# Lower query parts in both halves of the partitions, and score products over 128 rows, in a two-layer diffusion step on one Trainium2 core

## The chip, the core and the metric

The kernel runs on one core of one Trainium2 chip. The core has a matrix engine (TensorE; the profile calls its products PE and its weight loads PEld), a vector engine (DVE), a scalar engine (ACT), a general engine (POOL) and a queue engine (SP) that here issues nearly all transfers between the chip's memory and the core's on-chip memory. The on-chip memory has 128 partitions. The metric is the device time of one execution in microseconds (us).

## The reference: what is computed

One step of a small diffusion backbone in float32: 256 prompt tokens and 2048 sample tokens (a grid of 32 rows and 64 columns) with 1024 channels pass two layers. Layer 0 is a convolution branch, layer 1 an attention with 16 heads of 64 channels. The change touches the attention alone:

```python
# prompt: plain softmax attention of 256 tokens, per head
s = jnp.einsum('bqhd,bkhd->bhqk', qi, k).astype(jnp.float32)
p = jax.nn.softmax(s, axis=-1)
o = jnp.einsum('bhqk,bkhd->bqhd', p, v)

# sample: each block of 16 columns of a row sees 8 rows x 32 columns (a mask leaves 16) and 512 cached context keys
s_loc = jnp.einsum('bjqhd,brjkhd->bhjqrk', qb, k_blk)
s_loc = jnp.where(mask, s_loc + bias, NEG_INF)
s_ctx = jnp.einsum('bjqhd,blhd->bhjql', qb, k_ctx)
p = jax.nn.softmax(jnp.concatenate([s_loc, s_ctx], axis=-1), axis=-1)
o = p_loc @ v_blk + p_ctx @ v_ctx        # then gated by silu(z), projected, added to x, normalised
```

Every query is scaled by one over the root of 64, and the outputs are the two normalised activations and the prompt's new keys and values.

## The kernel before

**Numbers in two parts.** Products run in a float format that keeps fewer digits than float32. The kernel therefore splits an operand x into an upper part (x rounded to the format) and a lower part (what is left). A projection is three products: upper by upper, lower by upper, upper by lower.

For scores there are two products, because a head has only 64 channels and the array 128 rows. The keys of a head lie on all 128 partitions: the upper parts on 64, the lower parts on the other 64 (for odd heads the halves are exchanged). The upper parts of the head's queries, `hd.q`, are loaded from memory twice, into both halves of the partitions, so one product over 128 rows gives (upper queries) x (upper keys + lower keys). The lower parts of the queries, `hd.ql`, are loaded once for a pair of heads: the even head lies on partitions 0 to 63, the odd one on 64 to 127. The second product, line 1408, takes the 64 partitions of its head and the 64 partitions with the upper keys, and adds (lower queries) x (upper keys). In these products the queries are the weights that are loaded into the array, 128 queries at a time, and the keys stream through it.

**Stages.** Up to about 1800 us come the convolution layer and the projections of the attention layer (the queries' parts are written to memory as `qh_d` and `ql_d`). Then `phase2` does the attention. It goes twice over eight heads (a half); within a half first the prompt, two heads at a time (four prompt units), then four groups of eight grid rows, each with its eight heads. A sample head has four units of 128 queries (eight rows of one block of 16 columns). So there are 256 sample units and 8 prompt units.

**One unit** (`sample_unit`): scores against the 512 context keys (tile `ck`) and against a window of 11, 15, 15 or 12 key rows times 32 columns (tile `a_k`, read in a strided order; 352, 480, 480 or 384 columns), all into a score tile `sa_S` of which there are two; DVE takes the minimum and adds bias and mask (lines 1474 and 1476); ACT takes the exponential (1480), DVE the inverse of the sum (1481), POOL multiplies by it (1482); TensorE transposes the probabilities in eight pieces (1492); ACT copies them rounded (1501) and DVE forms the lower parts (109). Every second unit the value products follow (1517 to 1524), and between them, in pieces of six products, the output projection (1625 to 1627).

**Order.** `attention` runs the units as a pipeline. A step has the transposes of one unit, the softmax work of another, value products or a piece of the output projection, and then the scores of the next unit. TensorE and DVE keep the order in which the code is written (`manual_schedule`). ACT, POOL and SP are ordered by a scheduler with a time model of its own. `load_ahead` calls `load_head` one head ahead of use. The buffers that bear on this: keys `kt` two, upper queries `qh` two, lower queries `ql` two, bias `bm` two, values `vl` three. A load waits until the last reader of the buffer's former content is done, and SP issues its transfers one after the other, so a waiting one holds those behind it.

Of the kernel before, what the change touches and what calls it, by code (L numbers as in the profile page):

```python
# [52 lines left out]
# times of the start: of a weight's load, rounding and rest; of the first products; of the modulation; of the input rows  # L53
# [11 lines left out]
# per group of eight query rows: first key row, number of key rows  # L65
KEY_ROWS = [(0, 11), (4, 15), (12, 15), (20, 12)]
# and the key columns that share a product with the probabilities: ten where their rows fit the array, else eight
KEY_COLS = [10, 8, 8, 10]
# per block of 16 query columns: first key column / 8, kind of column window, first bias column
# [6 lines left out]
class Kern:  # L76
# [24 lines left out]
    # ---------------------------------------------------------------- helpers  # L101
# [15 lines left out]
    def slot(self, dt, name, shape, late=True):  # L117
        """16 KB per partition: of four that stay through phase 1 or of three that are given up before its end."""
        return self.sp.tile(shape, dt, tag="slot", name=name) if late else self.rp.tile(shape, dt, tag="slot", name=name, bufs=3)
# [10 lines left out]
    # -------------------------------------------------------------- constants  # L130
    def constants(self):
# [7 lines left out]
        # vectors over channels, one column per 128 channels  # L139
# [7 lines left out]
    def vectors(self, name, srcs, change=None):  # L147
        """Vectors over channels are loaded; the function returned puts them as columns of 128 channels."""
# [23 lines left out]
    def more_constants(self):  # L172
        """The other vectors, in two steps."""
        cp, io = self.cp, self.io
        columns = self.vectors("vecs", [io["norm_g"], io["ada_b"][0, : 2 * D]])
        yield
        vecs = columns()
        self.norm_g = [vecs[:, 0, :], vecs[:, 1, :]]
        self.ada_b = [vecs[:, 2, :], vecs[:, 3, :]]
        self.shift = [cp.tile([P, 2, NK], F32, tag=f"shift{i}", name=f"shift{i}") for i in range(2)]  # L180
        self.gs = [cp.tile([P, 2, NK], F32, tag=f"gs{i}", name=f"gs{i}") for i in range(2)]
        yield

    def conv_constants(self):
        """Depthwise taps, [channel, tap], in two steps."""
# [16 lines left out]
    def ada_chunk(self, i, c, late=True, early=False):  # L202
        """Columns c*512.. of the modulation of layer i for both groups, in steps: weights loaded, products (four at a
        time, each in its own 32 columns of the array), their sums, and the result put where it belongs."""
# [36 lines left out]
    def spread_row(self, tile, row):  # L241
        """A DRAM row on all partitions."""
# [3 lines left out]
    # ------------------------------------------------------------------- norm  # L246
# [38 lines left out]
    def modulated_steps(self, xts, layer, g, hi, lo, c0, name, rest, on_act=False, flush=(), wide=False):  # L285
        """Rows of xts (already scaled to unit rms), modulated, transposed and split, into columns c0.. of hi, lo."""
# [36 lines left out]
    # ------------------------------------------------------------ projections  # L323
    def weight(self, w, c0, name):
        """Columns c0..c0+128 of w, split."""
# [10 lines left out]
    def halves(self, src, shape, name):  # L336
        """A piece of a weight, rounded, and what is left of it."""
# [15 lines left out]
    # ------------------------------------------------------------- conv layer  # L353
    def conv_layer(self, part_a, part_b):
        """Input projection and depthwise convolution in two chunks of tokens; the second carries on where the first
        ends. Every operation is put at the time it is due by the tensor engine's rate, and all are issued in that
        order: the sums of the first taps of a channel tile run on Pool after its projection, those of the others on
        DVE after that. part_b are the blocks of the second chunk, made along the way."""
# [13 lines left out]
        for s in range(2 * NK):  # L372
# [93 lines left out]
            # the convolution, in two halves of the columns  # L466
# [48 lines left out]
            # the first half: Pool, then DVE in two sums; the second half: DVE, then Pool  # L515
# [28 lines left out]
        # the modulation and the input blocks of the first chunk  # L544
# [62 lines left out]
        # the norm of the first two tiles  # L607
# [13 lines left out]
        # the rest of the modulation, a part of it after each channel tile of the second chunk  # L621
# [5 lines left out]
        # the input blocks of the second chunk  # L627
# [38 lines left out]
    def norm_stages(self, src, t0, y, room=None, wide=False):  # L666
        """Layer norm, both SiLUs and their product of 128 tokens, in stages; appends split [channel, token] tiles to y.
        room has five [128, 8, 128] tiles to work in, for where the pools for that are not there yet."""
# [33 lines left out]
        # variance by token on the partitions, then its root's inverse spread over all partitions  # L702
# [34 lines left out]
    def out_weight(self, w, name, res):  # L737
        """w, split, as four tiles of 16 KB per partition: [hi, lo][half of the rows]; two steps for 128 rows."""
# [12 lines left out]
    def conv_out(self, w, blocks, ready, res=None):  # L751
        """Output projection and residual; with res also the modulated input of the next layer."""
# [43 lines left out]
    def conv_out_pipeline(self, w, blocks, ready, ahead, res):  # L796
        """Output projection, residual and modulated input of the next layer for blocks whose first tiles are ready;
        a step has the products of a tile, the first half of the norm of the second tile after it and the second half
        of the norm of the next one. Also the norm of the tiles ahead."""
# [127 lines left out]
    # -------------------------------------------------------- attention input  # L927
    def spread_bias(self):
        """The flat position bias, one copy per query of a tile, each shifted by the query's place in the bias."""
# [6 lines left out]
    def bias_rows(self, h):  # L936
        """Position bias of head h for every query of a tile, from row -4 and column -16 of the tile's first."""
# [4 lines left out]
    def na_values(self, blocks, then):  # L942
        """Values of some tokens, [token, channel]; then() where the weights that follow may be loaded."""
# [33 lines left out]
    def na_rest(self, blocks):  # L977
        """Keys, queries and gates of some tokens, [channel, token]."""
# [40 lines left out]
    def store_values(self, c, src, t0, pm):  # L1019
        """Values of four heads of 128 tokens as (hi, lo); those of the sample in the order (pair of columns, row, 2)."""  # L1020
# [21 lines left out]
    def masked_bias(self):  # L1042
        """Window mask less bias of every head, kind of row group and kind of column block: the scores are kept negated."""
# [20 lines left out]
    def windows(raw, at, R):  # L1064
        """[query, pair of columns, row, column]: 32 columns of R rows of the bias, which lie BIAS_COLS apart."""
# [3 lines left out]
    def store_q(self, dst, rows, src, t0, n, f):  # L1069
        """Columns of the sample are stored as (group of eight rows, j, row, 16)."""  # L1070
# [11 lines left out]
    def keys(self, ct, src, t0, n, pm, nm):  # L1082
        """Keys of two heads, stored as (hi, lo); those of odd heads as (lo, hi)."""
# [45 lines left out]
    def context_values(self):  # L1129
        """Cached values as (hi, lo)."""  # L1130
# [13 lines left out]
    def gated_weights(self):  # L1144
        """The weights of the last projection times the gate of either group, split."""
# [19 lines left out]
    # ------------------------------------------------------------------ phases  # L1165
    @staticmethod
    def weave(main, side, n):
        """main, with n steps of side (n may be a fraction) after each of its steps, and then the rest of side."""
# [53 lines left out]
    # ------------------------------------------------------- attention and out  # L1222
    def start_attention(self):
        """The pool of what heads load, and the loads of the first head."""
# [38 lines left out]
    def attention(self):  # L1263
        """All heads, as a pipeline of units: a step issues one stage of each of three units, sums of values or a part
        of the output projection, and what was put off from the steps before."""
# [69 lines left out]
    # ------------------------------------------------------------------- loads  # L1335
    def load_head(self, hd):
# [5 lines left out]
        if G is None:  # L1342
# [6 lines left out]
            hd.ql = T("ql", [P, n], F32R, nm + "_ql")  # L1349
            nc.sync.dma_start(hd.ql.bitcast(F32), self.ql_d[rows, a : a + n])  # L1350
# [14 lines left out]
        hd.q = T("qh", [P, n], F32R, nm + "_qh")  # L1365
        src = self.qh_d[h * DH : h * DH + DH, a : a + n]
        nc.sync.dma_start(hd.q.bitcast(F32), bass.AP(src.tensor, src.offset, [[0, 2], *src.ap]))
        if b == 0:
            hd.grp["ql"] = T("ql", [P, n], F32R, nm + "_ql")
            nc.sync.dma_start(hd.grp["ql"].bitcast(F32), self.ql_d[rows, a : a + n])  # L1370
        else:
            hd.z = T("z", [P, n], F32, nm + "_z")
            nc.sync.dma_start(hd.z, self.zn_d[rows, a : a + n])
        hd.ql = hd.grp["ql"]
# [3 lines left out]
    def load_context(self, ctx, h):  # L1378
        """The cached keys and values of a head."""
# [9 lines left out]
    def load_values(self, hd):  # L1389
        """The values of a head's key rows, in the chunks of the products."""  # L1390
# [13 lines left out]
    def scores(self, out, q, ql, k, odd):  # L1404
        """out = (hi + lo of the queries) times (hi + lo of the keys) without lo times lo."""
        half = slice(DH, P) if odd else slice(0, DH)
        self.nc.tensor.matmul(out, q, k, start=True, stop=False)  # L1407
        self.nc.tensor.matmul(out, ql[half], k[half], start=False, stop=True)  # L1408

    # ------------------------------------------------------------------- units  # L1410
    def prompt_unit(self, hd):
        """Softmax of the 256 prompt queries of two heads; transposed and split into hd.pt."""
# [322 lines left out]
```

## Time and profile before

| What | Value |
|---|---|
| median of 3 runs | 3113.68 us (3113.0 to 3121.12) |
| the profiled execution | its span, first to last instruction, is 3115.0 us, within the runs; nothing is recorded around it |
| PE, busy | 3005.0 us (96%) |
| PEld, busy | 2328.0 us (75%) |
| DVE, busy | 1857.6 us (60%) |
| ACT, busy | 1427.7 us (46%) |
| POOL, busy | 1538.2 us (49%) |
| transfers | 537.40 MB, mean 173 GB/s |
| products of line 1407, window | 256, mean 708 ns |
| products of line 1408, window | 256, mean 704 ns |

A row of the profile's groups names line, engine, operation, the tiles written and read, their shapes, the count, and the busy time. The digits of a shape such as 64*128 are the rows and columns of the array that a product uses. A row of the timeline gives start, duration, engine, line and operation. A product's end is modelled (products overlap in the array), so what a product costs is better read from one start to the next. "Issue" is idle time that no semaphore explains.

### The profile page before, as it was taken

The page shows a single profiled execution, that of the slowest core. Times are in us where ns is not written, and L with a number is a line of the kernel's source. Part 1 is how long each engine was busy: PE and PEld are TensorE (multiplying, and loading weights), DVE is VectorE, ACT ScalarE, POOL GpSimd, SP SyncE. Part 2 cuts the span into 40 slices and gives each one's busy share as a digit, 9 for nine tenths or more (in the row PEclk, how much of TensorE's full clock was granted, in tenths as well). Part 3 has the DMA queues.
Part 4 walks back from the last instruction along what each step waited for, and adds up shares of the span by engine and source line. Part 5 has one row for each costly group of instructions (what it writes and reads, how often), then busy time and mean ns, then how long its engine had stood idle before and what let it go on. Part 6 is the DMA issues. An engine that isn't in the chain of part 4 may idle for free. (4 is left out here: it accounts for less than half of the span.)

```text
span 3115.0 us, 45374 instructions
## 1 busy us (share of the span) xinstructions
PE 3005.0 (96%) x15951; PEld 2328.0 (75%) x15951; DVE 1857.6 (60%) x3126; ACT 1427.7 (46%) x2538; POOL 1538.2 (49%) x1775
## 2 busy tenths in 40 slices
PE   6999999998999999999999989999999999999998
PEld 4888877775778989999888856666666666666666
DVE  4789999988865000345652046656566656666665
ACT  4466566775533222422222145555555545555553
POOL 4688877886533433622333133444444444444443
PEclk9999999998999999999999979999999999999999
DMA  6242554564355544689998445755545456555442
GB/s 232 86 136 90 197 188 156 183 198 161 122 169 159 149 127 131 187 242 315 347 328 265 125 149 183 204 144 144 143 136 172 137 176 204 164 145 142 132 136 99
DMA packets 429373, 537.40 MB, mean 173 GB/s; under 512 B 42066, under 2 KB 304042, under 8 KB 429017
## 3 DMA queue, kind: packets, MB, share of 16 engines
q1 hardware_dynamic: 429008, 530.42, 55.0%
q10 hardware_dynamic: 136, 4.07, 0.3%
q8 instruction: 127, 2.08, 0.3%
q14 instruction: 102, 0.83, 0.1%
HBM read 351.34 MB, written 187.13 MB: 173 GB/s over the span
## 5 line engine op out<-in xcount | busy, mean ns | idle before, releaser
L1482 POOL TENSOR_SCALAR sa_p<-sa_p,sa_m 128x992 f32<-128x992 f32 (+2 forms) x256 | 288.2, 1126 | 528.9 <-DVE sa_m L1481 424.9
L1501 ACT CAST sa_pt<-sa_T 128x512 fp32r<-128x512 f32 (+2 forms) x512 | 276.0, 589 | 540.9 <-PE sa_T L1492 540.8
L500 DVE SCALAR_TENSOR_TENSOR cv<-u,dw,cv 128x640 f32<-128x640 f32 (+2 forms) x570 | 427.9, 822 | 3.8 <-ACT cv L496 2.9
L1474 DVE TENSOR_REDUCE sa_m<-sa_S 128x1 f32<-128x512 f32 x256 | 176.9, 691 | 403.3 <-PE sa_S L1408 390.1
L109 DVE TENSOR_TENSOR sa_pt<-sa_T,sa_pt 128x512 fp32r<-128x512 f32 (+2 forms) x512 | 329.2, 684 | 4.1 <-ACT sa_pt L1501 3.8
L349 PE MATMUL ci_ps<-h_s_hi,ci_wh 128*128 128x512 f32 x768 | 307.1, 400 | 2.0 <-DVE shift L237 1.0
L1492 PEld LDWEIGHTS sa_T<-ident,sa_p 128*128 128x128 f32 (+2 forms) x2048 | 221.5, 140 | 115.0 <-issue 57.3
L351 PE MATMUL ci_ps<-h_s_hi,ci_wl 128*128 128x512 f32 x768 | 303.2, 395 | 0.0
L350 PE MATMUL ci_ps<-h_s_lo,ci_wh 128*128 128x512 f32 x768 | 302.9, 394 | 0.0
L1492 PE MATMUL sa_T<-ident,sa_p 128*128 128x128 f32 (+2 forms) x2048 | 284.1, 282 | 0.9 <-DVE sa_pt L109 0.9
L1480 ACT ACTIVATE sa_p<-sa_S,sa_m 128x992 f32<-128x992 f32 (+2 forms) x256 | 269.4, 1052 | 7.6 <-DVE sa_m L1476 4.5
L481 POOL TENSOR_TENSOR cv_s<-cv_s,cv_p 128x519 f32<-128x519 f32 (+1 forms) x155 | 233.3, 1505 | 69.7 <-DVE cv_s L504 49.0
L478 ACT ACTIVATE cv_p<-u,dw 128x640 f32<-128x640 f32 (+2 forms) x326 | 240.9, 770 | 55.0 <-POOL cv_s L481 35.7
L481 POOL TENSOR_TENSOR cv_p<-cv_p,cv_p 128x520 f32<-128x520 f32 (+1 forms) x155 | 227.7, 1469 | 26.8 <-ACT cv_p L478 19.2
L1407 PE MATMUL sa_S<-a_k,a_qh 128*128 128x480 f32 (+2 forms) x256 | 181.3, 708 | 0.0
L1408 PE MATMUL sa_S<-a_k,a_ql 64*128 64x480 f32 (+2 forms) x256 | 180.3, 704 | 0.0
L1517 PE MATMUL sa_O<-sa_pt,cv 128*128 128x256 f32 x1024 | 177.1, 295 | 0.3 <-DVE 3_14_of L1538 0.3
L1476 DVE CUSTOM_DVE_ANT_0 sa_S<-sa_S,a_bm,sa_m 128x480 f32<-128x480 f32 (+2 forms) x256 | 170.9, 668 | 9.0
L349 PEld LDWEIGHTS ci_ps<-h_s_hi,ci_wh 128*128 128x128 f32 x768 | 145.5, 189 | 39.2 <-ACT cv_p L478 2.5
L351 PEld LDWEIGHTS ci_ps<-h_s_hi,ci_wl 128*128 128x128 f32 x768 | 145.1, 189 | 33.6
L350 PEld LDWEIGHTS ci_ps<-h_s_lo,ci_wh 128*128 128x128 f32 x768 | 145.4, 189 | 31.1
L106 POOL TENSOR_TENSOR nis_wl<-nis_w,nis_wh 128x1024 fp32r<-128x1024 f32 x24 | 60.9, 2540 | 183.0 <-ACT nis_wh L341 157.8
(846 smaller groups left out, 7495.5 us busy)
## 6 DMA issues: line engine op xcount, KB each, us to landing
adaw<-in_ada_w SPq DMA_DIRECT2D x24, 1024.0 KB
ci_w<-in_conv_w_in SPq DMA_DIRECT2D x48, 512.0 KB
a_bm<-bm_d SPq DMA_DIRECT2D x32, 720.0 KB
x_s<-in_x_sample SPq DMA_DIRECT2D x32, 512.0 KB
vs_d<-v_s SPq DMA_DIRECT2D x128, 128.0 KB
a_qh<-qh_d SPq DMA_DIRECT2D x64, 256.0 KB
o_x<-x_d SPq DMA_DIRECT2D x32, 512.0 KB
a_v<-vs_d SPq DMA_DIRECT2D x128, 120.0 KB
```

Of the source, the lines that this page charges most:

```text
L109: self.nc.vector.tensor_tensor(out=lo, in0=src, in1=hi.bitcast(F32), op=ALU.subtract)
L349: self.nc.tensor.matmul(out, wh[:, k, :], hh[:, k, :], start=k == 0, stop=False)
L350: self.nc.tensor.matmul(out, wh[:, k, :], hl[:, k, :], start=False, stop=False)
L351: self.nc.tensor.matmul(out, wl[:, k, :], hh[:, k, :], start=False, stop=k == NK - 1)
L478: nc.scalar.activation(t, st["u"][:, c0 + tap : c1 + tap], AF.Copy, scale=self.dw[:, ct, tap : tap + 1])
L481: nc.gpsimd.tensor_tensor(out=st["sum", half], in0=st["sum", half], in1=st[half, tap], op=ALU.add)
L500: nc.vector.scalar_tensor_tensor(out=out, in0=u, scalar=w, in1=first, op0=ALU.mult, op1=ALU.add)
L1407: self.nc.tensor.matmul(out, q, k, start=True, stop=False)
L1480: nc.scalar.activation(p[:, n], S[:, n], AF.Exp, scale=-1.0, bias=m[:, 2:3], accum_out=m[:, 3:4])
L1482: nc.gpsimd.tensor_scalar(out=p[:, n], in0=p[:, n], scalar1=m[:, 3:4], scalar2=1.0, op0=ALU.mult, op1=ALU.mult)
L1492: nc.tensor.transpose(t[:w, c * P : c * P + P], p[:, x + c * w : x + c * w + w], self.ident)
L1501: nc.scalar.copy(pt[:w, 0, part, :, at], t)
```

## The change

`load_head` now loads the lower parts of a head's queries as it loads the upper parts: twice, into both halves of the partitions, one tile per head. For the prompt, which takes two heads at once, the tile `ql` has two planes, and each head's plane is filled in both halves. `scores` no longer picks 64 partitions: its second product runs over all 128 rows, and gives (lower queries) x (upper keys + lower keys). The product of the two lower parts, which was left out before, is thereby included. The number of products, their columns and the weights' columns are as before; the tile `ql` takes the same space at most, 2 KB per partition. The load of the gate `hd.z` follows the load of `ql` for odd heads. The rest of the diff removes comments, which shifts line numbers by two from the loads on.

```diff
@@ load_head, prompt
-            hd.ql = T("ql", [P, n], F32R, nm + "_ql")
-            nc.sync.dma_start(hd.ql.bitcast(F32), self.ql_d[rows, a : a + n])
+            hd.ql = T("ql", [P, 2, NPR], F32R, nm + "_ql")
+            for e in range(2):
+                src = self.ql_d[(h + e) * DH : (h + e + 1) * DH, 0:NPR]
+                nc.sync.dma_start(hd.ql[:, e].bitcast(F32), bass.AP(src.tensor, src.offset, [[0, 2], *src.ap]))
@@ load_head, sample
-        hd.q = T("qh", [P, n], F32R, nm + "_qh")
-        src = self.qh_d[h * DH : h * DH + DH, a : a + n]
-        nc.sync.dma_start(hd.q.bitcast(F32), bass.AP(src.tensor, src.offset, [[0, 2], *src.ap]))
-        if b == 0:
-            hd.grp["ql"] = T("ql", [P, n], F32R, nm + "_ql")
-            nc.sync.dma_start(hd.grp["ql"].bitcast(F32), self.ql_d[rows, a : a + n])
-        else:
+        hd.q, hd.ql = (T(t, [P, n], F32R, f"{nm}_{t}") for t in ("qh", "ql"))
+        for t, d in ((hd.q, self.qh_d), (hd.ql, self.ql_d)):
+            src = d[h * DH : h * DH + DH, a : a + n]
+            nc.sync.dma_start(t.bitcast(F32), bass.AP(src.tensor, src.offset, [[0, 2], *src.ap]))
+        if b:
             hd.z = T("z", [P, n], F32, nm + "_z")
             nc.sync.dma_start(hd.z, self.zn_d[rows, a : a + n])
-        hd.ql = hd.grp["ql"]
@@ scores
-    def scores(self, out, q, ql, k, odd):
-        half = slice(DH, P) if odd else slice(0, DH)
+    def scores(self, out, q, ql, k):
         self.nc.tensor.matmul(out, q, k, start=True, stop=False)
-        self.nc.tensor.matmul(out, ql[half], k[half], start=False, stop=True)
+        self.nc.tensor.matmul(out, ql, k, start=False, stop=True)
@@ sample_unit (prompt_unit likewise)
-        self.scores(ctx, hd.q[:, cs], hd.ql[:, cs], hd.ctx[h][0], b)
-        self.scores(loc, hd.q[:, cs], hd.ql[:, cs], kw, b)
+        self.scores(ctx, hd.q[:, cs], hd.ql[:, cs], hd.ctx[h][0])
+        self.scores(loc, hd.q[:, cs], hd.ql[:, cs], kw)
```

TensorE's order stays as it was, and only the second products' weights are other tiles. The place is unit 0 of sample head 1 with the transposes around it; `a_0` and `a_1` are the tiles of heads 0 and 1. Before:

```order
L1407 MATMUL sa_1_0_S<-ck_16372,a_1_qh 128x512
L1408 MATMUL sa_1_0_S<-ck_16372,a_0_ql 128x512
L1407 MATMUL sa_1_0_S<-a_1_k,a_1_qh 128x352
L1408 MATMUL sa_1_0_S<-a_1_k,a_0_ql 128x352
L1492 MATMUL sa_0_2_T_17069<-ident,sa_0_2_p 128x128 x4
L1492 MATMUL sa_0_2_T_17074<-ident,sa_0_2_p 110x128 x4
```

After:

```order
L1405 MATMUL sa_1_0_S<-ck_16374,a_1_qh 128x512
L1406 MATMUL sa_1_0_S<-ck_16374,a_1_ql 128x512
L1405 MATMUL sa_1_0_S<-a_1_k,a_1_qh 128x352
L1406 MATMUL sa_1_0_S<-a_1_k,a_1_ql 128x352
L1490 MATMUL sa_0_2_T_17075<-ident,sa_0_2_p 128x128 x4
L1490 MATMUL sa_0_2_T_17080<-ident,sa_0_2_p 110x128 x4
```

The odd head reads a lower-query tile of its own, `a_1_ql`, where it read the even head's. DVE's order does not change at all; ACT and POOL each have one pair of neighbouring operations exchanged.

SP's order is rewritten by the scheduler. The place is the loads of sample head 4 in the second group of rows (`a_4_k` its keys, `a_4_bm` its bias, `a_4_v` its values). Before:

```order
L1364 DMA a_3_bm<-bm_d 128x1440
L1397 DMA a_3_v<-vs_d 30x8x128
L1370 DMA a_4_ql<-ql_d 128x512
L1397 DMA a_4_v<-vs_d 30x8x128 x2
L1359 DMA a_4_k<-ks_d 128x960
L1367 DMA a_4_qh<-qh_d 128x1x512
L1397 DMA a_4_v<-vs_d 30x8x128
L1364 DMA a_4_bm<-bm_d 128x1440
L1397 DMA a_4_v<-vs_d 30x8x128
L1655 DMA x_d<-o_0_0_x 128x1024
```

After:

```order
L1366 DMA a_3_bm<-bm_d 128x1440
L1396 DMA a_3_v<-vs_d 30x8x128 x2
L1396 DMA a_4_v<-vs_d 30x8x128 x2
L1361 DMA a_4_k<-ks_d 128x960
L1370 DMA a_4_qh<-qh_d 128x1x512
L1370 DMA a_4_ql<-ql_d 128x1x512
L1366 DMA a_4_bm<-bm_d 128x1440
L1396 DMA a_4_v<-vs_d 30x8x128 x2
L1653 DMA x_d<-o_0_0_x 128x1024
```

The lower queries' load went from ahead of the head's values to right behind the upper queries, for every head and no longer for even heads alone; the bias and the last two value loads come behind it.

A third place is where the first half's sample heads begin, behind the prompt's loads (`aNone`). Before:

```order
L1348 DMA aNone_qh<-qh_d 128x1x256 x2
L1350 DMA aNone_ql<-ql_d 128x256
L1367 DMA a_0_qh<-qh_d 128x1x512
L1359 DMA a_0_k<-ks_d 128x704
L1370 DMA a_0_ql<-ql_d 128x512
L1384 DMA ck_17231<-kc_d 128x512
L1386 DMA cv_17233<-cvs_d 128x4x128
L1384 DMA ck_17398<-kc_d 128x512
L1359 DMA a_1_k<-ks_d 128x704
```

After:

```order
L1348 DMA aNone_qh<-qh_d 128x1x256 x2
L1352 DMA aNone_ql<-ql_d 128x1x256 x2
L1361 DMA a_0_k<-ks_d 128x704
L1370 DMA a_0_qh<-qh_d 128x1x512
L1370 DMA a_0_ql<-ql_d 128x1x512
L1361 DMA a_1_k<-ks_d 128x704
L1370 DMA a_1_qh<-qh_d 128x1x512
L1370 DMA a_1_ql<-ql_d 128x1x512
L1383 DMA ck_17239<-kc_d 128x512
```

The prompt pair has two lower-query loads, and the loads of head 1 moved ahead of the cached keys and values (`ck`, `cv`) of later heads.

More of the change, by code (lines that the diff above doesn't have):

```diff
@@ L1418, in prompt_unit @@
                 cs = slice(u * P, u * P + P)
-                self.scores(S[:, (2 * e + u) * NPR : (2 * e + u + 1) * NPR], hd.q[:, e, cs], hd.ql[:, cs], hd.k[:, e], e)
+                self.scores(S[:, (2 * e + u) * NPR : (2 * e + u + 1) * NPR], hd.q[:, e, cs], hd.ql[:, e, cs], hd.k[:, e])
         yield
```

## The prediction

> **What bounds the kernel now.** I read the profile from the whole to the single instruction. The page gives a span of 3115.0 us; the list of stretches says which engine is full in the part that the change touches; the list of waits says whether that engine ever stands still for another; the timeline of TensorE (PE its products, PEld its weight loads) says what its time goes into.
>
> ```profile
> span 3115.0 us, 45374 instructions
> ...
> 2000.00:2200.00 200.00, 198.65 (x987) 129.32 (x987) 120.96 (x258) 103.16 (x186) 84.66 (x121) 1.00 0.52 144
> ...
> 1826.91 0.39 PE L1407 MATMUL sa_S<-ck,a_qh 128*128 128x512 f32 x1
> ...
> PE sa_S L1407 <- DMA a_qh<-qh_d: 5.6, 1, 5.6
> ...
> PE sa_S L1408 <- DMA a_ql<-ql_d: 0.4, 1, 0.4
> ```
>
> The columns of the second row are the stretch, its length, the busy time of PE, PEld, DVE, ACT and POOL, the granted clock, the DMA share and GB/s. PE is busy 198.65 of 200 us at full clock, DVE 121, ACT 103, POOL 85, and the DMA engines 0.52 of their time. The sample's attention runs from 1826.91 to the end, 1288 us for 256 units (two halves of eight heads, four groups of rows, four blocks of columns), 5.0 us each. In all of it PE waits for a score's query loads 6.0 us. So PE's own time per unit sets the end, and the question is what is inside it. Here are the four score products of one unit (lower and upper queries against the context, then against the window), with the weight loads that precede them:
>
> ```profile
> 2003.12 0.19 PEld L1407 LDWEIGHTS sa_S<-ck,a_qh 128*128 128x128 f32 x1
> 2003.23 0.39 PE L1407 MATMUL sa_S<-ck,a_qh 128*128 128x512 f32 x1
> 2003.55 0.18 PEld L1408 LDWEIGHTS sa_S<-ck,a_ql 64*128 64x128 f32 x1 [0.25 <-issue]
> 2003.55 0.50 PE L1408 MATMUL sa_S<-ck,a_ql 64*128 64x512 f32 x1
> 2003.98 0.19 PEld L1407 LDWEIGHTS sa_S<-a_k,a_qh 128*128 128x128 f32 x1 [0.25 <-issue]
> 2003.98 0.77 PE L1407 MATMUL sa_S<-a_k,a_qh 128*128 128x480 f32 x1
> 2004.68 0.18 PEld L1408 LDWEIGHTS sa_S<-a_k,a_ql 64*128 64x128 f32 x1 [0.51 <-issue]
> 2004.68 0.77 PE L1408 MATMUL sa_S<-a_k,a_ql 64*128 64x480 f32 x1
> 2005.38 0.85 PEld L1492 LDWEIGHTS sa_T<-ident,sa_p 128*128 128x128 f32 x8 [0.52 <-issue]
> 2005.38 1.09 PE L1492 MATMUL sa_T<-ident,sa_p 128*128 128x128 f32 x8
> ...
> 2006.23 0.72 PE L1517 MATMUL sa_O<-sa_pt,cv 128*128 128x256 f32 x4
> ```
>
> The ends of products are modelled, so I go by starts. The first weight load (2003.12) starts 0.11 us before its product: it lies under the product ahead. The next four, those into and out of the 64-row products, start at the same time as their own product: PEld stood idle 0.25 to 0.52 us, with nothing to wait for, and nothing was loaded ahead. From start to start the products take 0.32, 0.43, 0.70 and 0.70 us. Compare a row of products of the same kind, all of them 128 rows deep, each with other weights than the one before:
>
> ```profile
> 2101.39 0.40 PE L1625 MATMUL o<-w2h,0_1_y2h 128*128 128x512 f32 x1
> 2101.62 0.39 PE L1626 MATMUL o<-w2l,0_1_y2h 128*128 128x512 f32 x1
> 2101.85 0.40 PE L1627 MATMUL o<-w2h,0_1_y2l 128*128 128x512 f32 x1
> 2102.08 0.40 PE L1407 MATMUL sa_S<-ck,a_qh 128*128 128x512 f32 x1
> ...
> 2101.62 0.19 PEld L1627 LDWEIGHTS o<-w2h,0_1_y2l 128*128 128x128 f32 x1
> 2101.85 0.19 PEld L1407 LDWEIGHTS sa_S<-ck,a_qh 128*128 128x128 f32 x1
> ```
>
> A 512-column product costs 0.23 us here, and the load for the next one starts with the one before. So 0.09 us (0.32 - 0.23) passes after the first score product before the array takes the 64-row load, and 0.20 us (0.43 - 0.23) goes on the second: 0.11 us of its load, as the load's lead over its product shows elsewhere, and again 0.09 us.
>
> **The change part by part.** It takes the 64-row products away; their place is held by 128-row products of as many columns. What of the 0.09 and 0.11 us is the stream itself cannot change: a 64-row and a 128-row product of the strided 480 columns both take 0.70 us, so the rows add nothing. What goes, per unit:
>
> First product to second: 0.32 to 0.23, **0.09 us**. Second to third: 0.43 to 0.23, **0.20 us**. Third and fourth, against the strided window: their stream without load and wait is nowhere in the trace. From above, the overhead is that of the 512-column product, 0.20. From below I use the shorter window:
>
> ```profile
> 2603.01 0.63 PE L1407 MATMUL sa_S<-a_k,a_qh 128*128 128x352 f32 x1
> 2603.57 0.63 PE L1408 MATMUL sa_S<-a_k,a_ql 64*128 64x352 f32 x1
> 2604.13 1.09 PE L1492 MATMUL sa_T<-ident,sa_p 128*128 128x128 f32 x8
> ```
>
> 0.56 us for 352 columns and 0.70 for 480 is 0.0011 us a column; 480 columns are then 0.53 and the rest is 0.17, or 0.16 if the rounded starts hide 0.005 us. I take **0.18** for each of both. The transposes that follow are now led by a load that starts with its product (2005.38); eight of them take 0.85 us. With that load under the fourth product they lose between 0 and 0.11; they are limited by their own eight loads (PEld is busy 0.85 of these 0.85 us), of which only the start of the first moves, so I take half, **0.06**. Sum: 0.09 + 0.20 + 0.18 + 0.18 + 0.06 = 0.71 us a unit (bounds 0.09 + 0.20 + 0.16 + 0.16 = 0.61, and 0.09 + 0.20 + 0.20 + 0.20 + 0.11 = 0.80). Times 256 it is **182 us** (156 to 205).
>
> On what the 0.09 us is, two rules of the Trainium skill part ways. "TensorE: Matmul & The Clock Gate", step-by-step, lets one product's drain overlap the next one's fill, by which only the loads could be won, about 4 x 0.11 x 256 = 113 us by this trace's load. "TensorEngine Tiling (Array Packing)", Key Properties, has every change of the tiling mode drain the array, and 64 rows after 128 are such a change. The 0.32 us row is with the second.
>
> The prompt's eight units have 32 such pairs with 256 columns. They start at half clock behind their loads:
>
> ```profile
> L1408 PE MATMUL pa_S<-aNone_k,aNone_ql x16: 378/579/580, 1800.4 to 1823.2; 64*128 64x256 f32 x16
> ...
> 1800.00:1850.00 50.00, 37.33 (x130) 24.58 (x130) 21.41 (x42) 21.38 (x59) 15.22 (x34) 0.66 0.56 165
> ```
>
> PE is busy 37 of 50 us there, at a clock of 0.66. A pair can save 0.09 + 0.20 = 0.29, 32 pairs 9 us; where PE waits for loads it saves nothing. I take **5 us** (0 to 9).
>
> What is added are loads. The lower queries of a sample head pair were one load of 256 KB; now each head has its own of 256 KB, and each prompt pair two of 128 KB for one:
>
> ```profile
> a_ql<-ql_d SPq DMA_DIRECT2D x31, 256.0 KB
> ...
> L1370 SPq DMA_DIRECT2D a_ql<-ql_d x32: 422/979/2467, 1817.2 to 3008.8; - x32
> L1367 SPq DMA_DIRECT2D a_qh<-qh_d x64: 503/526/597, 1816.1 to 3033.7; - x64
> ...
> SPq L1359 <- PE sa_S L1408: 30.2, 29, 1.2
> ```
>
> That is 32 more sample loads and 8 more prompt loads, 9.4 MB. SP's queue spends about 0.5 us on each, as on an upper-query load. At 144 GB/s and a share of 0.52 the engines would move 277 GB/s full, so a load of 256 KB is 1.0 us of them, 34 us in all, where 0.48 x 1288 = 618 us are free. The loads are hidden by the head ahead: SP issues the keys of the next head when the last score product of the head before the present one has released their buffer (the last row; there are two), so a head's whole time, 4 x 5.0 = 20 us, before they are needed. After the change that is 4 x 4.3 = 17 us, still more than twice the time that the about 2.2 MB of a head take at 277 GB/s (8 us). Where the cover is thin, at the first prompt and sample heads of both halves, an extra load is 1.5 us late (0.5 + 1.0), and it can be late some three times. I take **4 us lost** (0 to 15).
>
> The buffers of the lower queries now turn over per head, as those of the upper queries do; they are released by the same products, so no new wait is queued on SP, only a row behind one that already waits. PE and DVE keep their order; DVE has the next largest need per unit:
>
> ```profile
> L109 DVE TENSOR_TENSOR sa_pt<-sa_T,sa_pt 128x512 fp32r<-128x512 f32 (+2 forms) x512 | 329.2, 684 | 4.1 <-ACT sa_pt L1501 3.8
> L1474 DVE TENSOR_REDUCE sa_m<-sa_S 128x1 f32<-128x512 f32 x256 | 176.9, 691 | 403.3 <-PE sa_S L1408 390.1 <-POOL o_r L252 4.4 <-POOL 1_1_y2h L103 2.2
> L1476 DVE CUSTOM_DVE_ANT_0 sa_S<-sa_S,a_bm,sa_m 128x480 f32<-128x480 f32 (+2 forms) x256 | 170.9, 668 | 9.0
> L1481 DVE RECIPROCAL sa_m<-sa_m 128x1 f32<-128x1 f32 x256 | 42.0, 164 | 39.0 <-ACT sa_p L1480 26.5
> ```
>
> 0.691 + 0.668 + 0.164 + 2 x 0.684 = 2.9 us. PE's mean step falls from 5.0 to 4.3, still above. Only a step of scores and transposes alone (2.15 + 0.85 = 3.0, then 2.3) falls below; nearly every step has value products (1.1 to 2.3 us more) or six output products (1.4 us), since 256 steps share 128 first halves of value products, 64 second halves that come a step later and 144 pieces of the output projection, and the two score buffers let DVE lag by part of a unit. For an estimated dozen bare steps at 0.6 us, 7 us in all, of which the buffers hide some, I take **5 us lost** (0 to 9).
>
> Sum: 3115.0 - 182 - 5 + 4 + 5 = 2937 us for the profiled execution. The runs' median, 3113.68, lies 1.3 us under its span, so the forecast is **2936 us**. By the bounds: 3115 - 205 - 9 - 1 = 2900 to 3115 - 156 + 15 + 9 - 1 = 2982.
>
> **The rivals.** *DVE takes over.* If every second step were bare, DVE's 2.9 us against 2.3 would cost 128 x 0.6 = 77 us instead of 5: 2936 + 72 = 3008 us. For it speaks that DVE waits 390 us for scores now, which says that it follows PE closely; against it that this waiting, 1.5 us a unit, is twice what PE gives up.
>
> *The loads stay in the open.* If a load could not go under a product that uses the same rows, whatever their number, the four would still start with their products, nothing would be won, and 4 us of loads be lost: 3118 us. The rows at 2101.62 and 2101.85 speak against it: full-row loads under full-row products. "TensorE: Matmul & The Clock Gate" (packing, the mechanism) states this rule, that loads overlap only products of other row groups; in its second part it also allows a load into the background buffer. The rows named agree with the latter.
>
> *Slower: transfers are the real pace.* The attention moves 144 GB/s in the stretch shown, at 1288 us some 186 MB. If that were all these short packets could have, 9.4 MB more would take 65 us more, and no saving on PE would show: 3180 us. It decides once a head's loads last longer than its 17 us. The share of 0.52 and the 6.0 us that PE waited for queries speak against it.
>
> **How the numbers follow.** Forecast 0.86, DVE 0.08, loads in the open 0.03, transfers 0.03. A difference of 0.3% (9 us) is about what a measurement of this kernel can tell from none. Faster holds the first two, 0.94; same is the third, 0.03; slower the last, 0.03. The range is the forecast's own bounds, 2900 to 2982; beside the other cases' 0.14 some 0.05 of the forecast's chance lies outside.
>
> **What would show it.** In the changed profile the second and fourth score products should read 128*128, their loads start with the product ahead (not with their own), starts lie 0.23, 0.23, about 0.52 and 0.52 us apart for 480 columns, and idle "issue" time of the weight loads on the two score lines vanish. PE should stay above 95% busy between 2000 and 2200, DVE rise to about 0.70. It would be wrong if the loads keep starting with their products, if PE's idle time before transposes grows behind DVE, or if query, key or value loads show up as PE's waits by tens of us.

## The result: slower by 6.9%

| | median | ratio to before, 95% interval |
|---|---|---|
| before, in the same session | 3114.71 us | |
| the change | 3327.51 us (3326.82 to 3331.55) | 1.0686 [1.0671, 1.0701] |

The forecast was 2936 us. The kernel lost 213 us where it was to gain 178. Every ratio in this document is to the kernel before in the same session; over the three sessions that kernel took 3114.7, 3110.1 and 3113.6 us. Here are the span and the stretch between 2000 and 2200 us of the changed kernel (the columns are those of the stretch shown of before), then what TensorE waited for from 1780 us on (us in total, how often, the longest):

```profile
span 3329.8 us, 45406 instructions
...
2000.00:2200.00 200.00, 157.33 (x836) 124.99 (x835) 105.27 (x223) 88.62 (x159) 71.38 (x107) 0.86 0.55 154
...
PE sa_S L1406 <- DMA a_ql<-ql_d: 206.1, 48, 7.9
PE sa_S L1405 <- DMA a_qh<-qh_d: 49.0, 19, 9.1
PE pa_S L1406 <- DMA aNone_ql<-ql_d: 38.0, 12, 5.6
PE pa_S L1405 <- DMA aNone_k<-ks_d: 13.4, 2, 7.1
PE pa_O L1450 <- DMA aNone_v<-vp_d: 7.2, 2, 4.6
```

PE is busy 157 of 200 us where it was busy 199, and its clock fell from 1.00 to 0.86. 48 times it waits for the lower queries (206 us), 19 times for the upper ones (49 us). The first of these waits hardly existed before (0.4 us). The share of the 16 DMA engines is 0.55, hardly more than the 0.52 of before.

The products themselves became as fast as foreseen. One unit in the timeline of the changed kernel, where nothing is waited for:

```profile
2209.03 0.19 PEld L1405 LDWEIGHTS sa_S<-ck,a_qh 128*128 128x128 f32 x1
2209.15 0.40 PE L1405 MATMUL sa_S<-ck,a_qh 128*128 128x512 f32 x1
2209.15 0.19 PEld L1406 LDWEIGHTS sa_S<-ck,a_ql 128*128 128x128 f32 x1
2209.38 0.40 PE L1406 MATMUL sa_S<-ck,a_ql 128*128 128x512 f32 x1
2209.38 0.19 PEld L1405 LDWEIGHTS sa_S<-a_k,a_qh 128*128 128x128 f32 x1
2209.62 0.70 PE L1405 MATMUL sa_S<-a_k,a_qh 128*128 128x480 f32 x1
2209.62 0.19 PEld L1406 LDWEIGHTS sa_S<-a_k,a_ql 128*128 128x128 f32 x1
2210.12 0.73 PE L1406 MATMUL sa_S<-a_k,a_ql 128*128 128x480 f32 x1
...
2210.66 1.06 PE L1490 MATMUL sa_T<-ident,sa_p 128*128 128x128 f32 x8
...
2211.48 0.48 PE L1623 MATMUL o<-w2h,0_1_y3h 128*128 128x512 f32 x1
```

Every load starts with the product ahead. The starts lie 0.23, 0.24, 0.50 and 0.54 us apart, 1.51 us for the 2.15 us of before; the median of the 128 units with 480 columns is 1.49 us. So the place where the time went is not the product but what it waits for. At the turn to the next head, in the timelines of SP and PE:

```profile
2209.96 0.51 SPq L1370 DMA_DIRECT2D a_qh<-qh_d  x1
2210.53 0.87 SPq L1370 DMA_DIRECT2D a_ql<-ql_d  x1
...
2222.04 0.47 PE L1405 MATMUL sa_S<-ck,a_qh 128*128 128x512 f32 x1 [0.61 <-ACT sa_p L1478]
2227.86 0.79 PE L1406 MATMUL sa_S<-ck,a_ql 128*128 128x512 f32 x1 [5.34 <-DMA a_ql<-ql_d]
```

The lower queries are issued at 2210.53 and are there at 2227.8, 17 us later, for 256 KB. The view of the transfers for two of these microseconds, when little else was under way (packets, bytes, then the queue's share of the 16 engines):

```profile
DMA packets 48, 0.10 MB, mean 49 GB/s; under 512 B 2, under 2 KB 2, under 8 KB 48
...
q1 hardware_dynamic: 48, 0.10, 12.5%
```

A share of 12.5% of 16 engines is two engines. 46 of the 48 packets are rows of queries of 2 KB (512 numbers of 4 bytes); in the packet records they take 0.084 to 0.094 us each when alone, mostly 0.084. A doubled load is 128 such packets: by estimate 128 x 0.085 / 2 = 5.4 us on two engines, and not the 1.0 us that the prediction worked out for sixteen. Both doubled loads of a head run on them one after the other: in the packet records the 256 query packets of this head run from 2215.2 to 2227.3 us, 128 of them up to 2221.0. So twelve of the 17 us go to these two loads; in the five before them only packets of other transfers run.

### The profile page after: what moved, and what is told of

The parts are those of the page before. It is cut to its first block, busy times and chain, and to the rows that moved or that the text cites. A ratio compares the mean times of both kernels' runs of the same rounds, so it can differ in the third digit from the quotient of the medians.

```text
span 3329.8 us, 45406 instructions
## 1 busy us (share of the span) xinstructions
PE 2910.5 (87%) x15951; PEld 2423.1 (73%) x15951; DVE 1865.4 (56%) x3126; ACT 1444.8 (43%) x2538; POOL 1535.9 (46%) x1775
## 5 line engine op out<-in xcount | busy, mean ns | idle before, releaser
L1490 PEld LDWEIGHTS sa_T<-ident,sa_p 128*128 128x128 f32 (+2 forms) x2048 | 280.2, 157 | 140.8 <-issue 119.4
L1490 PE MATMUL sa_T<-ident,sa_p 128*128 128x128 f32 (+2 forms) x2048 | 307.1, 298 | 7.0 <-POOL sa_p L1480 3.7
L1406 PE MATMUL sa_S<-ck,a_ql 128*128 128x512 f32 x256 | 117.5, 459 | 206.3 <-DMA a_ql<-ql_d 206.1
L1406 PEld LDWEIGHTS sa_S<-ck,a_ql 128*128 128x128 f32 x256 | 52.5, 205 | 228.8 <-DMA a_ql<-ql_d 226.0
L1515 PE MATMUL sa_O<-sa_pt,cv 128*128 128x256 f32 x1024 | 197.8, 321 | 0.3 <-DVE 3_14_of L1536 0.3
L1406 PE MATMUL sa_S<-a_k,a_ql 128*128 128x480 f32 (+2 forms) x256 | 166.8, 652 | 0.0
```

What stands on the lines that cost most here:

```text
L1406: self.nc.tensor.matmul(out, ql, k, start=False, stop=True)
L1490: nc.tensor.transpose(t[:w, c * P : c * P + P], p[:, x + c * w : x + c * w + w], self.ident)
```

## The experiments

**Theory A**: a transfer that reads its 64 rows twice in one go is carried by two of the sixteen engines, and two such loads per head make those two the pace of the attention. **Rival B**: the loads are issued too late, because the buffer of the lower queries now turns over per head and SP's one queue holds them back. The first three kernels undo the changed kernel's loads and products one by one; the fourth is the kernel before with one load split.

### Both query loads split

The products stay; each doubled load becomes two plain ones.

```diff
+    def both_halves(self, t, src):
+        for s in range(2):
+            self.nc.sync.dma_start(t[s * DH : (s + 1) * DH].bitcast(F32), src)
 ...
         for t, d in ((hd.q, self.qh_d), (hd.ql, self.ql_d)):
-            src = d[h * DH : h * DH + DH, a : a + n]
-            nc.sync.dma_start(t.bitcast(F32), bass.AP(src.tensor, src.offset, [[0, 2], *src.ap]))
+            self.both_halves(t, d[h * DH : h * DH + DH, a : a + n])
```

> The changed kernel, but the upper and the lower queries of a head are each loaded by two plain transfers of 64 rows, one per half of the partitions, in place of one transfer that reads the 64 rows twice. Products, buffers and bytes stay as in the changed kernel; SP issues one more transfer per load. Theory A (a transfer that reads its rows twice runs on two of the sixteen DMA engines, 128 packets of 0.085 us, 5.5 us each; two per head make these two engines the pace): the loads spread over all engines, TensorE no longer waits for the lower queries, about 2936 us (2900 to 2982), PE busy over 95% between 2000 and 2200 us. Rival B (the loads are issued too late, because the lower queries' buffer now turns over per head in SP's one queue, and the bias waits ahead of the values): nothing of that is changed, 3300 us or more.

Measured: 2930.06 us, ratio 0.9423 [0.9408, 0.9438]. The stretch and the waits:

```profile
2000.00:2200.00 200.00, 198.30 (x1146) 155.63 (x1144) 138.77 (x296) 120.36 (x214) 93.14 (x126) 1.00 0.66 171
...
PE sa_S L1409 <- DMA a_ql<-ql_d: 6.3, 4, 2.6
```

PE is full again, and the wait for the lower queries fell from 206 to 6 us with the same bytes, buffers and products. The order on SP is not quite the same: the lower queries now go out behind the bias, which is later and not earlier.

```profile
2109.73 0.50 SPq L1370 DMA_DIRECT2D a_bm<-bm_d  x1
2110.28 1.08 SPq L1338 DMA_DIRECT2D a_ql<-ql_d  x2
```

Rival B falls. (The run with four parts, below, leaves SP's order exactly as in the changed kernel and is faster too.) This kernel is 5.8% faster than before and the fastest of all that ran.

### Only the lower queries split

```diff
-        for t, d in ((hd.q, self.qh_d), (hd.ql, self.ql_d)):
-            src = d[h * DH : h * DH + DH, a : a + n]
-            nc.sync.dma_start(t.bitcast(F32), bass.AP(src.tensor, src.offset, [[0, 2], *src.ap]))
+        src = self.qh_d[h * DH : h * DH + DH, a : a + n]
+        nc.sync.dma_start(hd.q.bitcast(F32), bass.AP(src.tensor, src.offset, [[0, 2], *src.ap]))
+        self.both_halves(hd.ql, self.ql_d[h * DH : h * DH + DH, a : a + n])
```

> The changed kernel, but only the lower queries are loaded by two plain transfers of 64 rows; the upper queries keep the one transfer that reads its rows twice, as before the change. Theory A: the two engines carry 10.5 us of other work and one doubled load of 5.5 us per head, 16 us, against a head's 17.2 us on TensorE: nearly free, 2936 to 3000 us. Rival B: 3300 us or more.

Measured: 3065.75 us, ratio 0.9861 [0.9846, 0.9877]. I expected it nearly free, and it gives back 136 us of the split kernel's gain. The waits are fewer, not gone:

```profile
PE sa_S L1410 <- DMA a_ql<-ql_d: 48.1, 24, 5.5
PE sa_S L1409 <- DMA a_qh<-qh_d: 36.5, 12, 10.5
```

One doubled load per head, which costs little at 20 us a head (30 us in all, by the fourth kernel), costs more at 17: I take it that a mean of 16 us of work on two engines, by my estimate, does not fit into 17 us when loads are waited for one by one. No run tests this by itself. The direction is A's, the size was mine to miss.

### The loads alone

The changed kernel's loads; the second product over 64 rows.

```diff
+        half = slice(DH, P) if odd else slice(0, DH)
 ...
-        self.nc.tensor.matmul(out, ql, k, start=False, stop=True)
+        self.nc.tensor.matmul(out, ql[half], k[half], start=False, stop=True)
```

> The changed kernel's loads, but the second score product runs over 64 rows as before (half of what is loaded of the lower queries is not read). Theory A: the two engines need about 20.5 us per head (10.5 + 11 less the plain load that fell away), 64 heads from 1845 us on give 3157 us or more; with the waits of the changed kernel, whose pace they set, 3300 to 3400 us; TensorE's waits for queries stay, its starts are again 0.32, 0.43, 0.70, 0.70 us apart. If the waits came from TensorE's faster pace alone, with 20 us a head as before they would go: 3115 to 3130 us. Rival B: as slow as the changed kernel or slower, so this run does not tell A from B.

Measured: 3330.05 us, ratio 1.0713 [1.0695, 1.0731].

```profile
PE sa_S L1407 <- DMA a_ql<-ql_d: 110.4, 30, 7.1
PE pa_S L1407 <- DMA aNone_ql<-ql_d: 28.7, 11, 5.6
PE sa_S L1406 <- DMA a_qh<-qh_d: 13.5, 6, 5.8
PE pa_S L1406 <- DMA aNone_k<-ks_d: 6.9, 1, 6.9
```

The same time as with the faster products, to 0.3%: PE's work per unit fell by 0.6 us from this kernel to the changed one, some 160 us in all, and its waits for queries and the prompt's keys grew by nearly as much, from 160 us (these four lines) to 307 (the first four lines of the changed kernel). That is what a pace set elsewhere looks like. By the starts of the heads' first products, the second group of eight heads takes 179 us here and 182 us in the changed kernel, 22.6 us a head, where A's two engines need 20.5 by an estimate: 0.52 of a head's 20 us, the mean load of every engine before the change, less 0.7 us for the doubled load in it, and two loads of 5.4 us. In the changed kernel's packet records there is hardly a moment (1.5% of the time from 1850 to 3000 us) with no packet under way; before the change it was 9%, in the split kernel 13% (to 2900 us). And in 34% of the time, from 1850 us to 150 us before the end, just one or two packets are under way, as two engines alone would leave it; before the change it was 18%, in the split kernel 5%. So the two are short of throughput; whether the 2 us between 20.5 and 22.6 are packets slowed by others was not separated.

### The kernel before, upper queries split

```diff
 ...
-        nc.sync.dma_start(hd.q.bitcast(F32), bass.AP(src.tensor, src.offset, [[0, 2], *src.ap]))
+        self.both_halves(hd.q, src)
```

> The kernel before, but the upper queries are loaded by two plain transfers of 64 rows in place of one that reads its rows twice. Theory A: before the change the two engines had 15 to 16 us of work in a head's 20 us and nobody waited: no change but the few us of waits for queries, 3105 to 3115 us. Rival B: the same. It shows whether the split gains by itself.

Measured: 3079.74 us, ratio 0.9904 [0.9888, 0.992]. I expected no change; it gains 30 us. Here are the stretches of this kernel where the gain lies; of before, the first is in the prediction (37.33 us busy, clock 0.66), and the second stands last here:

```profile
1800.00:1850.00 50.00, 46.88 (x203) 30.62 (x203) 33.27 (x71) 30.44 (x77) 21.54 (x48) 0.83 0.70 204
...
1900.00:2000.00 100.00, 100.00 (x507) 65.74 (x508) 63.44 (x138) 52.90 (x99) 40.99 (x64) 1.00 0.63 181
```

```profile
1900.00:2000.00 100.00, 94.40 (x469) 63.94 (x469) 60.06 (x133) 48.82 (x94) 39.44 (x68) 0.95 0.68 210
```

Before the change the two engines already cost time, nearly all of it where the first half begins: the first group of heads took 150 us and takes 130 now, the first sample product starts 9 us earlier. The listed waits for queries (6 us) hid this, because they count neither the prompt's waits nor the lower clock that follows them.

### Other rows, and four parts

Is it the count of two that confines the transfer, or the reading of the same rows twice? One kernel takes the second 64 rows from another head; the other takes 32 rows of each of four heads. Both so compute the scores of other data, with the same amount of work; they are there for their time alone.

```diff
 ...
+        src = d[min(h, NH - 3) * DH : min(h, NH - 3) * DH + DH, cols]
+        self.nc.sync.dma_start(t.bitcast(F32), bass.AP(src.tensor, src.offset, [[2 * DH * NTOK, 2], *src.ap]))
```

```diff
 ...
+        src = d[min(h, NH - 7) * DH : min(h, NH - 7) * DH + DH // 2, cols]
+        self.nc.sync.dma_start(t.bitcast(F32), bass.AP(src.tensor, src.offset, [[2 * DH * NTOK, 4], *src.ap]))
```

> The changed kernel, but each doubled query load takes its second 64 rows not from the same rows again but from the head after the next (one transfer still, its outer count still two, the same bytes and packets). The lower half of the partitions so holds another head's queries; the scores are those of other data, the amount of work is the same. Theory A1 (the outer count of two puts the transfer on two engines): as slow as the changed kernel, 3300 to 3350 us, 24 packets of 2 KB per us while these loads run alone. Rival A2 (reading the same rows twice is what is slow): about 2930 us, as with the split loads.

> As the run with other rows, but each query load takes 32 rows of each of four heads in one transfer: an outer count of four, the same 128 rows of 2 KB. The scores are again those of other data with the same amount of work. Theory A1: four engines, about 48 packets per us when alone, 2.8 us a load; these engines then carry 10.5 - 1.0 + 5.5 = 15 us in a head's 17 us: 2930 to 2990 us. If the number of engines were always two or the cost lay elsewhere: 3300 us.

Measured: 3327.39 us (1.0688 [1.0667, 1.071]) with two parts of other rows, 3012.09 us (0.9675 [0.9656, 0.9695]) with four parts, two runs of each. The waits of the first, then a microsecond of the second in which almost only query rows run:

```profile
PE sa_S L1410 <- DMA a_ql<-ql_d: 206.6, 49, 7.9
PE sa_S L1409 <- DMA a_qh<-qh_d: 48.0, 19, 8.0
```

```profile
DMA packets 41, 0.09 MB, mean 90 GB/s; under 512 B 0, under 2 KB 0, under 8 KB 40
...
q1 hardware_dynamic: 40, 0.08, 24.0%
```

With other rows the time and the waits are as with the same rows, to the microsecond. With an outer count of four the share is 24%, four engines, and 40 packets in this microsecond (48 in most others in which only query rows run) for 24. SP issues its transfers in exactly the same order in both kernels and in the changed one, so the 315 us between them cannot come from the order of issue. For these two counts the outer count of the access pattern is thus the number of engines. The rule stands in the Trainium skill, "DMA: Bandwidth & Descriptors" (why a DMA increments its semaphore by 16, how many engines): the number of engines is the largest up to 16 that divides the slowest dimension of both access patterns. The same page of the Trainium skill, in its rules for kernel authors, names this very case, a leading zero-stride broadcast of c copies on at most c engines. In the section on how many engines the Trainium skill also says that on these queues the lowest-numbered ones are taken, which would put all doubled loads on the same two. The runs agree with that, though the records do not number the engines: with both loads of a head issued the share was 12.5%, and the second load ran behind the first. Four parts took 3012 us where I expected 2930 to 2990: four engines at an estimated 15 of 17 us a head are still waited for.

### The products alone, and regrouped

The split loads with 64-row products price the products; the same with another order of the four products asks what it is that held the loads back.

```diff
-        self.scores(ctx, hd.q[:, cs], hd.ql[:, cs], hd.ctx[h][0], b)
-        self.scores(loc, hd.q[:, cs], hd.ql[:, cs], kw, b)
+        half = slice(DH, P) if b else slice(0, DH)
+        for out, k in ((ctx, hd.ctx[h][0]), (loc, kw)):
+            nc.tensor.matmul(out, hd.q[:, cs], k, start=True, stop=False)
+        for out, k in ((ctx, hd.ctx[h][0]), (loc, kw)):
+            nc.tensor.matmul(out, hd.ql[half, cs], k[half], start=False, stop=True)
```

> The kernel with both query loads split (2930 us), but the second score product runs over 64 rows as before the change; half of the lower queries loaded is not read. It prices the products alone, with the same loads. Theory P (changes between 64 and 128 rows leave the loads in the open and drain the array, 0.64 us a unit as the group times 155 and 134 us per 32 units say): starts 0.33, 0.43, 0.70, 0.70 us apart, 3080 us (3070 to 3095). Rival (a part of the gain of the split kernel came from its loads' order): 3000 to 3050 us.

> The run before with the four score products in another order: both 128-row products first (context, window), then both 64-row products (context, window). Nothing is left out. Theory M (it is the change of the number of rows that drains the array and holds the next load back): two changes a unit in place of four; starts 0.23, 0.59, 0.34, 0.59 us apart, 1.75 for 2.15 us, 256 x 0.40 = 102 us faster than the run before, about 2980 us. Rival R (a load for a 64-row product, or behind one, is never taken ahead): 0.23, 0.59, 0.43, 0.70, 1.95 us, 51 us faster, about 3030 us.

Measured: 3088.68 us (0.992 [0.9905, 0.9935]) with 64-row products, 3004.94 us (0.9644 [0.9621, 0.9666]) regrouped. The first lies in P's range of 3070 to 3095 us, and its starts are those of before, 2.15 us for the four. The products alone are worth 3088.68 - 2930.06 = 158.6 us, 0.62 us a unit; the two kernels ran in different sessions, and with each counted from before in its own it is 155 us. A unit of the regrouped kernel:

```profile
2103.89 0.39 PE L1474 MATMUL sa_S<-ck,a_qh 128*128 128x512 f32 x1
2103.89 0.19 PEld L1474 LDWEIGHTS sa_S<-a_k,a_qh 128*128 128x128 f32 x1
2104.12 0.69 PE L1474 MATMUL sa_S<-a_k,a_qh 128*128 128x480 f32 x1
2104.74 0.18 PEld L1476 LDWEIGHTS sa_S<-ck,a_ql 64*128 64x128 f32 x1 [0.66 <-issue]
2104.74 0.49 PE L1476 MATMUL sa_S<-ck,a_ql 64*128 64x512 f32 x1
2104.85 0.19 PEld L1476 LDWEIGHTS sa_S<-a_k,a_ql 64*128 64x128 f32 x1
2105.08 0.68 PE L1476 MATMUL sa_S<-a_k,a_ql 64*128 64x480 f32 x1
2105.69 0.85 PEld L1497 LDWEIGHTS sa_T<-ident,sa_p 128*128 128x128 f32 x8 [0.65 <-issue]
```

The load of the second 64-row product (2104.85) starts 0.23 us ahead of it, under the first 64-row product. Only the two changes of the number of rows, 128 to 64 at 2104.74 and back at 2105.69, have a load that starts with its product. Starts are 0.23, 0.62, 0.34 and 0.61 us apart, 1.80 for 2.15 us; 84 us were gained, nearer M's 102 than R's 51, and the load under a 64-row product is what R excludes. The 0.59 us that I gave a strided product before a change is 0.62: after the strided stream of 0.50 us, 0.12 us pass until the array takes the next load, not 0.09.

## Why the prediction was wrong

**The products: right.** Their term was 182 us (156 to 205), 0.71 us a unit. By the median starts of all units the split kernel saves 0.66 us a unit on the four score products, and the eight transposes take 0.83 us for 0.85, 0.02 us where 0.06 were counted; that makes 174 us. In time the products are worth 155 to 159 us, at the lower bound. The difference is about what PE's gaps grew by: from the first sample product on they sum to 34 us in the split kernel and to 14 us with the 64-row products.

The Trainium skill's two rules on the drain were weighed rightly: 155 us and more came, where the loads alone would give 113 by the prediction's count, and the pause stands only where the number of rows changes between 128 and 64, as "TensorEngine Tiling (Array Packing)", Key Properties, has it. The rule of the Trainium skill ("TensorE: Matmul & The Clock Gate", packing, the mechanism) that a load goes only under a product of other row groups is refuted twice here, by full rows under full rows (starts 0.23 us apart) and by 64 rows under 64 (the load 0.23 us ahead of its product).

**The loads: wrong, and this decided.** The step that failed: "At 144 GB/s and a share of 0.52 the engines would move 277 GB/s full, so a load of 256 KB is 1.0 us of them". It took the sixteen engines as one pool. The doubled load has two of them, and takes 5.4 us. The next step, "still more than twice the time that the about 2.2 MB of a head take at 277 GB/s (8 us)", fails with it: two engines had about 20.5 us of work per head, against 17. The term "4 us lost (0 to 15)" measured 3327.5 - 2930.1 = 397 us (393 with each counted from before in its own session), the price of the doubled form of both loads. The trace of before showed it to whoever looked at the packets: its upper-query loads have the same form, and when alone run at 23 to 24 packets of 2 KB a microsecond, two engines' worth. A mean share of 0.52 said nothing on the two. The step "no new wait is queued on SP" does not hold either: the bias loads wait 196 us there (19 us before). I take it to follow from the late queries, since with the same order and four engines no line of this wait reaches 12 us.

**The rivals.** "Transfers are the real pace" had the right engine and the right sign, at 0.03, but was priced by bytes (3180 us) and dismissed by the mean share and by PE's waits in the old kernel, whose pace still hid most of them. The prediction's own sign of being wrong, query loads among PE's waits by tens of us, is what came. DVE did not take over: in the split kernel it is busy 139 of 200 us, near the 0.70 foreseen, and the 5 us for it need no correction that the runs could show.

**The sum without that step.** With both loads spread, the same kernel takes 2930 us, against a forecast of 2936. Part of this agreement is luck: the products gave 23 to 27 us less than their term, and splitting the upper queries gave about as much (25 and 30 us, from before to the two kernels with split loads and 64-row products) that the forecast did not contain.

## What to carry to other kernels

A transfer's cost in these runs is its packets divided by the engines that it really uses, and with outer counts of two and four these were two and four: look at the share of the engines in a window where one kind of load runs alone, before a mean share is taken as room. Products of unequal row counts are best put next to their like, since here each change between 128 and 64 rows left a weight load in the open. And an engine made faster takes away the time that hid everything loaded for it: compare the new pace with each load's own time, not with the old waits.

## What was not expected of the hardware

A doubled load of 256 KB took 5.4 us on two engines by estimate, about 6 us in the packet records of the head shown, and copying the rows by two plain transfers of 64 rows removed nearly all waits, 397 us of 3327, at the price of one more issue on SP. A rule of the Trainium skill's page "DMA: Bandwidth & Descriptors" advises against two transfers to the two halves of the partitions, since both spread over all engines, and for one of 128 partitions. No run here compares them with one plain transfer of 128 rows; against one that is confined to two engines the two transfers won by 397 us.

Waits cost twice. In the changed kernel PE's gaps from the first sample product on sum to 310 us (26 us before), and the granted clock falls with them: 0.80 to 0.92 between 1900 and 3200 us, where before it was 0.95 to 1.00.

The change of the row count costs 0.09 us after a contiguous stream of 512 columns, beside the load in the open, and 0.12 us after a strided one whose own load lay ahead (0.62 - 0.50). In the kernel before, where that load lay in the open too, both together cost 0.20 us (0.70 - 0.50) and not 0.11 + 0.12; why is open. Rows fewer than 128 alone do not cost this: products of 110 and 120 rows stand next to 128-row products at 0.12 us a start, as 128-row products of 256 columns do.
